# A trunk layer on one core: who adds the plain banks to the residual, the order of the next pair's loads, and where the weight sums pause

## The chip, the core and the metric

The kernel runs on one core of a Trainium2 chip. The metric is the time of one execution on the device in microseconds, lower is better. The core has five engines that run side by side, each with an instruction queue of its own that it works through in order: TensorE (PE in the profile; its weight loads are PEld), VectorE (DVE), ScalarE (ACT), GpSimd (POOL) and SyncE (SP), which here only starts transfers. An instruction waits in its queue until the semaphores of what it needs have come, and everything behind it on that engine waits too. Transfers that SP starts go through one queue (q1 in the profile), those that GpSimd starts through another (q0), and both share 16 DMA engines. Some of GpSimd's add to what is in the target (accumulating transfers).

## The reference, cut to what matters

The reference is one layer of a language model over 272 positions (16 meta tokens and 256 others), all in float32: a mixer (retention heads beside mLSTM heads), then a feed-forward part, then a last norm. The change lies in the feed-forward part:

```python
h = h + mix                                   # 272 x 2048
u = rmsnorm(h, norm_ffn)
up = causal_dwconv(u @ w_up, ffn_conv_w, ffn_conv_b)   # w_up: 2048 x 11264
gate, val = jnp.split(up, [5632], axis=-1)
h = h + (jax.nn.silu(gate) * val) @ w_down    # w_down: 5632 x 2048
return rmsnorm(h, norm_final)[:, 16:]         # 256 x 2048
```

## The kernel before

Float32 products are made of three reduced-precision ones. Every weight tile is loaded raw (`wraw`), ScalarE casts it to its high part `whi`, VectorE subtracts to get the rest `wlo` (together a split), and TensorE multiplies the activations' high part with both and their low part with `whi`. `whi` and `wlo` rotate through five buffers each, `wraw` through two homes of two tiles (`wraw0`, `wraw1`). Lines 140 and 142 (`split_w`) and 766 and 768 (`split`) are these splits.

Up to about 719 us the kernel makes the projections of the mixer (108 loads), its output (32 loads) and the first half of `w_up` (88 loads); a counter, `paced`, counts these loads. Then the last product follows for the first half of the 5632 rows of `w_down` (719 to 838 us), then the other 88 loads of `w_up`, then the second half of `w_down` (from 1091 us). I call the two `half` 0 and 1.

In one half the product with `w_down` runs over two pairs of column blocks of 512 (`b` = 0 and 2), and in each over eleven steps `q` of 256 rows each. Every step treats 2 tiles of 128 tokens and 2 blocks. Steps 0, 9 and 10 are plain: four products, 24 matmuls of 512 columns, accumulated into four PSUM banks `cs` (`atps` in the profile). Steps 1 to 8 use a scheme of seven products instead of eight for a 2 x 2 block product (`seven`, 21 matmuls): three into the banks `cs`, four into four more banks `ps` (`mmps`). VectorE makes one difference of weight tiles per step (line 830, `ta`) and four splits. The third combination of weight tiles, a sum of several, is not made on an engine: it is prepared in DRAM ahead of time.

These weight sums (class `Early`) are prepared while the projections run. Each of the 29 units has four parts: a copy of 512 KB from DRAM to DRAM (line 203, SP), and three accumulating transfers of 256 KB (lines 214 and 216, GpSimd). Which part starts after which load is set by the table `ahead`: part i after load 40 + 38 i / 16.

When the last seven-product step of a pair is done, `share` empties the four banks `ps`: it makes four combinations with ScalarE and VectorE in tiles of `x5` and adds each to its block of the residual `hn` by an accumulating transfer (`onto`, line 863). After the pair's last plain step ScalarE copies the four `cs` banks to tiles of `x5` (line 1000), and `onto` adds these to the same four blocks, but for the last pair of all, where VectorE adds straight from the banks. A copied bank is free for the next pair's plain step 0. The copies reuse tiles of `share`: the second to the fourth wait until its first to third transfer have landed.

The loads of the next steps are written into the same loop: `load_plain` (two raw tiles of 512 KB into a home of `wraw`) and `load_seven` (512 KB, 256 KB, and 256 KB of the prepared sum, into one of two buffers `left` made of `hT`). All go through SP's queue in the order written, by `load`. At a pair's end that is: step 10's plain tiles after step 8, step (2,2)'s after it, and after step 9 the next pair's plain step 0. A scheduler in the framework then orders each engine's instructions by its own estimate of times, so a change of the source also moves others.

Of the kernel before, what the change touches and what calls it, by code (L numbers as in the profile page):

```python
# [33 lines left out]
W0 = GW + 2 * P  # L34
WARM = 8

AHEAD, AHEAD_STEP = 40, 38

# [45 lines left out]
def trunk(ctx: ExitStack, tc: tile.TileContext, io, out: bass.AP):  # L86
    nc = tc.nc
# [132 lines left out]
    early = {u: Early(*u) for u in units}  # L220

    ahead = sorted((4 * n + 3 * i, n, i) for n in range(len(units)) for i in range(4))
    ahead = [(AHEAD + AHEAD_STEP * i // 16, early[units[n]].parts[p]) for i, (_, n, p) in enumerate(ahead)]


    mixp_cm = pool("mixp", 1, side="left")
# [530 lines left out]
    for half in range(2):  # L757
# [100 lines left out]
        def block(tt, b):  # L858
            return hn[:, tt, b * 512 : (b + 1) * 512]
# [49 lines left out]
        def load_plain(b, q, side, n=2):  # L909
            for j in range(b, b + n):  # L910
                raws[j, q] = raw_home([P, 2, 512], side)
                load(raws[j, q], io["wd"][j, half * NQD + q])

        def load_seven(b, q):

            nonlocal turn
            raw = left[turn]
            turn = 1 - turn
            load(raw[:, 2:4, :], io["wd7"][b // 2, half * NQD + q][:, 2:4, :])
            load(raw[:, 1, :], io["wd7"][b // 2, half * NQD + q][:, 1, :])  # L920
            load(raw[:, 0, :], early[b, half * NQD + q].kept[:, 0, :])
            homes[b, q] = raw
# [14 lines left out]
        for b in (0, 2):  # L937
            cs = {}
            for j in range(2):
                for tt in range(2):  # L940
                    cs[tt, j] = at.tile([P, 512], F32, name="atps")
            ps = [mm.tile([P, 512], F32, name="mmps") for _ in range(4)]

            final = half == 1 and b == 2
            steps = [0, 1, 6, 2, 7, 3, 4, 5, 8, 9, 10] if final else range(NQD)
            fast = [q for q in steps if q in FAST and not (final and q in BOTH)]
            plain = [q for q in steps if q not in fast]
            alone = plain[-lag:] if final else []
            if b == 0:
                load_plain(b, 0, 0)  # L950
                load_seven(b, 1)
                load_seven(b, 2)
            sums_home = [raw_home([P, 2, 512], 1) for _ in range(2)]
            load_sum(b, 1)
            load_sum(b, 2)
            for q in steps:
                if q in fast:
                    due = []
                    if final and q != fast[0]:
                        due, gains = gains[:1], gains[1:]  # L960
                    seven(b, q, cs, ps, q == fast[0], q == fast[-1], emptied, due)
                    if q == fast[-1]:
                        with tc.high_priority() if final else nullcontext():
                            shared = share(ps, b, final)
                else:
                    for j in range(1 if q in alone else 2):
                        w = split_step(raws.pop((b + j, q)))
                        for tt in range(2):
                            product(cs[tt, j], tt, q, w, q == plain[0], q == plain[-1 - (lag if final and (tt, j) == (1, 1) else 0)])

                if final:
                    if q == 0:
                        load_plain(b, 6, 0)
                    elif q == 6:
                        load_plain(b, 7, 0, 1)
                    elif q in (3, 4, 5):
                        load_plain(b, q + 5, 0 if q < 5 else 1, 1)
                    if q in (1, 2, 3):
                        load_seven(b, q + 2)
                        load_sum(b, q + 2)  # L980
                else:
                    if q == 6:
                        load_plain(b, 9, 0)
                    if q in range(1, 7):
                        load_seven(b, q + 2)
                        load_sum(b, q + 2)
                    if q == 8:
                        load_plain(b, 10, 1)
                    if b == 0:
                        if q in (7, 8):  # L990
                            load_seven(2, q - 6)
                        elif q == 9:
                            load_plain(2, 0, 0)
            for j in range(2):
                for n, tt in enumerate(range(2)):
                    c = (b + j) * 512
                    if not final:

                        x = x_tile((4, 3, 1, 0)[2 * j + n])
                        emptied = nc.scalar.copy(x, cs[tt, j])  # L1000
                        onto(tt, b + j, x)
                        if half == 1:
                            gains.append((tt, b + j, c, c + 512))
                    elif j == 0:
                        add(cs[tt, j], tt, c)
                        squares(tt, b, c, c + 512)
                        times_gain(tt, c, c + 512)
# [111 lines left out]
```

## Time and profile before

| what | value |
| --- | --- |
| median of 3 runs | 1219.86 us (1217.63 to 1221.83) |
| profiled execution, its own time | 1222.59 us |
| its span, first to last instruction | 1220.8 us |
| mean granted TensorE clock | 0.994 |
| instructions | 23064 |
| read from and written to memory | 268.59 MB, 42.47 MB |

Line 1000 runs twelve times, first at 776.6 and last at 1154.4 us; line 863 issues 27 transfers, 256 KB each, with a median of 8.3 us from issue to landing. In a row of the timeline the columns are: start and length in us, engine, line, operation, what it writes and reads, how often, and in brackets how long the engine had been idle before it and what ended that. In a row of a line's view the three numbers after the name are the shortest, median and longest length in ns, then come the first and the last start in us. In a row of waits stand the total in us, the number of waits and the longest. In a row of stretches stand, for each engine, the busy us and the number of instructions, then the granted clock, the busy share of the DMA engines and what they moved. Several matmuls overlap, so the distance between starts is what one costs, not its length.

### The profile page before, as it was taken

What the parts mean: (1) busy time and instruction counts of PE and PEld (TensorE: products, weight loads), DVE (VectorE), ACT (ScalarE), POOL (GpSimd) and SP (SyncE); (2) the same over time, 40 slices, a digit from 0 to 9 for tenths busy, and PEclk for the clock granted to TensorE, in tenths of its full rate; (3) what the DMA queues carried; (4) which work ended last, traced back from release to release, by engine and by line L of the source; (5) the groups of instructions that cost most, each with busy time, mean ns of one, the idle gap of its engine ahead of it and who ended that gap; (6) DMA issues with size and microseconds to landing.
All of it is one profiled execution on the core that took longest, in us unless ns stands there. A gap on an engine that the chain in (4) does not pass through costs nothing.

```text
span 1220.8 us, 23064 instructions
## 1 busy us (share of the span) xinstructions
PE 1202.5 (99%) x8947; PEld 1154.5 (95%) x8947; DVE 943.0 (77%) x1378; ACT 712.9 (58%) x973; POOL 270.1 (22%) x361
## 2 busy tenths in 40 slices
PE   9999999999999999999999999999999999999897
PEld 9999999999999999999999998788999999998686
DVE  8877878767765766788888779795877777779686
ACT  8657756656557556555555556564655555556573
POOL 0100022222221331232213200303232232210232
PEclk9999999999999999999999999999999999999899
DMA  8764677777886877778777867969988778858866
GB/s 276 269 214 157 209 231 216 236 217 223 235 234 179 260 231 222 227 245 243 222 229 223 234 198 250 268 216 284 275 264 243 222 230 224 227 183 290 236 205 181
DMA packets 104094, 281.64 MB, mean 231 GB/s; under 512 B 16624, under 2 KB 20848, under 8 KB 103856
## 3 DMA queue, kind: packets, MB, share of 16 engines
q1 hardware_dynamic: 84016, 239.06, 57.7%
q0 software_dynamic: 19392, 40.26, 18.5%
q8 instruction: 70, 1.15, 0.4%
q10 hardware_dynamic: 576, 0.85, 0.2%
q14 instruction: 40, 0.33, 0.1%
HBM read 268.59 MB, written 42.47 MB: 255 GB/s over the span
## 4 chain that ended last, share of the span: by engine, by line
PE 94%; DMA 4%; DVE 1%; ACT 1%; issue 0%; DVEq 0%; SPq 0%; ACTq 0%
PE mmps L149 25%; PE mmps L152 25%; PE mmps L150 25%; DMA wraw<-in_wd 2%; PE mmps L844 2%; PE mmps L845 2%; PE mmps L847 2%; PE atps L845 1%; PE atps L844 1%; PE atps L819 1%; PE atps L822 1%; PE atps L820 1%; PE atps L847 1%; DMA wraw<-in_wu 1%; DMA hT<-kept 1%; PE atps L442 1%
## 5 line engine op out<-in xcount | busy, mean ns | idle before, releaser
L140 ACT CAST whi<-wraw 128x1024 fp32r<-128x1024 f32 x346 | 361.9, 1049 | 355.8 <-PE mmps L150 226.9
L142 DVE TENSOR_TENSOR wlo<-wraw,whi 128x1024 fp32r<-128x1024 f32 x346 | 429.9, 1244 | 104.4 <-ACT whi L140 99.4
L149 PE MATMUL mmps<-uh,whi 128*128 128x258 f32 x1408 | 345.2, 283 | 2.9 <-ACT whi L140 2.9
L150 PE MATMUL mmps<-ul,whi 128*128 128x258 f32 x1408 | 344.9, 281 | 0.0
L149 PEld LDWEIGHTS mmps<-uh,whi 128*128 128x128 f32 x1408 | 265.3, 188 | 3.3 <-ACT whi L140 3.1
L150 PEld LDWEIGHTS mmps<-ul,whi 128*128 128x128 f32 x1408 | 266.8, 190 | 0.1
L149 PE MATMUL mmps<-xh,whi 128*128 128x272 f32 (+2 forms) x864 | 219.8, 288 | 0.0
L150 PE MATMUL mmps<-xl,whi 128*128 128x272 f32 (+2 forms) x864 | 218.4, 285 | 0.0
L152 PE MATMUL mmps<-uh,wlo 128*128 128x258 f32 x1408 | 197.9, 283 | 0.0
L152 PEld LDWEIGHTS mmps<-uh,wlo 128*128 128x128 f32 x1408 | 181.6, 190 | 0.0
L150 PEld LDWEIGHTS mmps<-xl,whi 128*128 128x128 f32 x864 | 162.8, 188 | 0.0
L149 PEld LDWEIGHTS mmps<-xh,whi 128*128 128x128 f32 x864 | 162.7, 188 | 0.1
L209 POOL TENSOR_TENSOR pace<-whi 128x1 f32<-128x1 f32 x87 | 52.0, 598 | 407.4 <-ACT whi L140 407.4
L152 PE MATMUL mmps<-xh,wlo 128*128 128x272 f32 (+2 forms) x864 | 126.9, 285 | 0.0
L152 PEld LDWEIGHTS mmps<-xh,wlo 128*128 128x128 f32 x864 | 114.6, 188 | 0.0
L695 DVE TENSOR_TENSOR cu<-mmps,rstd 128x258 f32<-128x258 f32 x88 | 37.5, 426 | 68.9 <-PE mmps L152 68.4
L768 DVE TENSOR_TENSOR wlo<-hT,whi 128x1024 fp32r<-128x1024 f32 x58 | 71.3, 1247 | 6.5 <-ACT whi L766 6.2
L766 ACT CAST whi<-hT 128x1024 fp32r<-128x1024 f32 x58 | 59.7, 1050 | 15.2 <-DMA hT<-kept 4.6
L766 ACT CAST whi<-wraw 128x1024 fp32r<-128x1024 f32 (+1 forms) x58 | 46.6, 836 | 32.7 <-DVE wraw L830 21.4
L150 PE MATMUL mmps<-mixl,whi 128*128 128x258 f32 x256 | 63.1, 283 | 0.0
L149 PE MATMUL mmps<-mixh,whi 128*128 128x258 f32 x256 | 62.5, 283 | 0.0
L768 DVE TENSOR_TENSOR wlo<-wraw,whi 128x1024 fp32r<-128x1024 f32 (+1 forms) x58 | 53.2, 953 | 1.9 <-PE mmps L847 0.8
(271 smaller groups left out, 1775.7 us busy)
## 6 DMA issues: line engine op xcount, KB each, us to landing
wraw<-in_wu SPq DMA_DIRECT2D x176, 512.0 KB, 4.5
wraw<-in_wi SPq DMA_DIRECT2D x108, 512.0 KB, 4.4
wraw<-in_wo SPq DMA_DIRECT2D x32, 512.0 KB, 4.5
wraw<-in_wd SPq DMA_DIRECT2D x30, 512.0 KB, 6.0
kept<-in_wd SPq DMA_DIRECT2D x29, 512.0 KB, 6.5
kept<-in_wd POOLq DMA_DIRECT2D x58, 256.0 KB, 6.3
hT<-in_wd SPq DMA_DIRECT2D x29, 512.0 KB, 5.1
kept<-kept POOLq DMA_DIRECT2D x29, 256.0 KB, 5.3
```

Of the source, the lines that this page charges most:

```text
L140: nc.scalar.copy(hi, raw)
L142: nc.vector.tensor_tensor(out=lo, in0=raw, in1=hi.bitcast(F32), op=ALU.subtract)
L149: nc.tensor.matmul(ps, hi[:, k, :], xh(kk), start=kk == first, stop=False)
L150: nc.tensor.matmul(ps, hi[:, k, :], xl(kk), start=False, stop=False)
L152: nc.tensor.matmul(ps, lo[:, k, :], xh(kk), start=False, stop=kk == last)
L209: with tc.issue_after(nc.gpsimd.tensor_tensor(out=pace, in0=x, in1=x, op=ALU.add).ins):
L695: evacuated = nc.vector.tensor_tensor(out=u, in0=ps[:, :NQ], in1=rstd2, op=ALU.mult)
L766: copied = nc.scalar.copy(hi, x)
L768: return copied, nc.vector.tensor_tensor(out=lo, in0=x, in1=hi.bitcast(F32), op=ALU.subtract)
L844: nc.tensor.matmul(o, sh[:, f, m, :], hi[:, i, :], start=begin, stop=False)
L845: nc.tensor.matmul(o, sl[:, f, m, :], hi[:, i, :], start=False, stop=False)
L847: nc.tensor.matmul(o, sh[:, f, m, :], lo[:, i, :], start=False, stop=end)
```

## The change

Three edits. First, after a pair's last plain step the copies are added to `hn` by VectorE, no longer by accumulating transfers. Second, in the first pair's loop, the loads of step (2,2) are written after those of the next pair's plain step 0, not before. Third, the table of the weight sums: parts start every 22 / 10 loads instead of every 38 / 16, and what would come at load 222 or later comes 16 loads later, so that no part starts between loads 222 and 238. The border of the halves is load 228.

```diff
-AHEAD, AHEAD_STEP = 40, 38
+AHEAD, AHEAD_STEP, REST, RESUME = 40, 22, 222, 238
...
-    ahead = [(AHEAD + AHEAD_STEP * i // 16, early[units[n]].parts[p]) for i, (_, n, p) in enumerate(ahead)]
+    at_load = (AHEAD + AHEAD_STEP * i // 10 for i in range(len(ahead)))
+    ahead = [(a if a < REST else a + RESUME - REST, early[units[n]].parts[p]) for a, (_, n, p) in zip(at_load, ahead)]
...
                     if b == 0:
-                        if q in (7, 8):
-                            load_seven(2, q - 6)
+                        if q == 7:
+                            load_seven(2, 1)
                         elif q == 9:
                             load_plain(2, 0, 0)
+                            load_seven(2, 2)
...
                         emptied = nc.scalar.copy(x, cs[tt, j])
-                        onto(tt, b + j, x)
+                        nc.vector.tensor_tensor(out=block(tt, b + j), in0=block(tt, b + j), in1=x, op=ALU.add)
```

What this does to the engines' order is shown at three places. Lines behind the table are numbered one or two higher in the new kernel, those behind the copies three higher.

SP's queue in half 0 at the end of the first pair, before: `wraw1` are the plain tiles of step 10, `wraw0` those of the next pair's step 0, and the three rows of `hT` step (2,2), the last of them its prepared sum.

```order
L907 DMA wraw1_9517<-in_wd 128x1024
L907 DMA wraw1_9519<-in_wd 128x1024
L907 DMA hT_72<-in_wd7 128x1024
L907 DMA hT_72<-in_wd7 128x512
L907 DMA hT_72<-kept2_2_89 128x512
L907 DMA wraw0_9556<-in_wd 128x1024
L907 DMA wraw0_9558<-in_wd 128x1024
```

And of the change:

```order
L909 DMA wraw1_9522<-in_wd 128x1024
L909 DMA wraw1_9524<-in_wd 128x1024
L909 DMA wraw0_9558<-in_wd 128x1024
L909 DMA wraw0_9560<-in_wd 128x1024
L909 DMA hT_72<-in_wd7 128x1024
L909 DMA hT_72<-in_wd7 128x512
L909 DMA hT_72<-kept2_2_89 128x512
```

The two plain tiles moved ahead of three transfers, 1 MB. The same holds in half 1.

VectorE's queue at the same border, before: the splits of the next pair's plain step 0 (`wraw0`), then those of step (2,1), whose `ta` stands ahead of them.

```order
L830 TENSOR_TENSOR wraw1_9608<-hT_72 128x1024
L142 TENSOR_TENSOR wlo_9614<-wraw0_9556,whi_9612 128x1024
L142 TENSOR_TENSOR wlo_9630<-wraw0_9558,whi_9628 128x1024
L768 TENSOR_TENSOR wlo_9646<-hT_72,whi_9645 128x1024
L768 TENSOR_TENSOR wlo_9656<-hT_72,whi_9655 128x1024
```

And of the change:

```order
L143 TENSOR_TENSOR wlo_9619<-wraw0_9558,whi_9617 128x1024
L832 TENSOR_TENSOR wraw1_9613<-hT_72 128x1024
L143 TENSOR_TENSOR wlo_9635<-wraw0_9560,whi_9633 128x1024
L1004 TENSOR_TENSOR hn_4814<-hn_4814,x5_5926 128x512 x4
L770 TENSOR_TENSOR wlo_9651<-hT_72,whi_9650 128x1024
L770 TENSOR_TENSOR wlo_9661<-hT_72,whi_9660 128x1024
```

The four adds stand between the splits of the plain step and those of step (2,1). Each waits for ScalarE's copy and for the landing of the transfer that `share` sent to the same block. On ScalarE the four copies now stand together behind both casts of the plain step; before, two stood between the casts and two behind.

SP's queue at the border of the halves, before: the last plain tiles, the first tiles of `w_up`'s second half, and the copy that begins a weight sum (`kept0_17`).

```order
L907 DMA wraw1_9985<-in_wd 128x1024
L907 DMA wraw1_9987<-in_wd 128x1024
L126 DMA wraw0_10066<-in_wu 128x1024
L126 DMA wraw0_10159<-in_wu 128x1024
L203 DMA kept0_17_101<-in_wd7 256x512
L126 DMA wraw1_10096<-in_wu 128x1024
L126 DMA wraw1_10129<-in_wu 128x1024
```

And of the change:

```order
L909 DMA wraw1_9990<-in_wd 128x1024
L909 DMA wraw1_9992<-in_wd 128x1024
L127 DMA wraw0_10071<-in_wu 128x1024
L127 DMA wraw0_10162<-in_wu 128x1024
L127 DMA wraw1_10101<-in_wu 128x1024
L127 DMA wraw1_10132<-in_wu 128x1024
```

The sum's copy is gone from there: it now starts ten loads before the half's end. The tile behind it, `wraw1_10096`, is the second that TensorE needs. GpSimd's three accumulating transfers of weight sums that were issued around this border move too, and so do the weight sums between all other loads.

## The prediction

> **What bounds the kernel now.** I read four views, in this order: the page (which engine is full), the list of waits of the matmul engine (when it is not full), a table by stretches around those waits, and the timeline at them. L-numbers are lines of the kernel before.
>
> ```profile
> PE 1202.5 (99%) x8947; PEld 1154.5 (95%) x8947; DVE 943.0 (77%) x1378; ACT 712.9 (58%) x973; POOL 270.1 (22%) x361
> PE atps L819 <- ACT x L1000: 5.9, 2, 3.8
> PE mmps L149 <- ACT whi L140: 2.9, 1, 2.9
> ```
>
> TensorE (PE) is busy for 99% of the span, so only what holds PE up can be won. Apart from the first microsecond and the tail there are three such places. I call them A, C and B: two waits for a copy out of a plain bank (L1000), 2.1 and 3.8 us, and one of 2.9 us for a split weight tile.
>
> ```profile
> core 0: us, PE busy (x) PEld busy (x) DVE busy (x) ACT busy (x) POOL busy (x), PEclk, DMA share, GB/s
> 400.00:420.00 20.00, 20.00 (x168) 20.00 (x168) 14.72 (x18) 10.12 (x14) 5.61 (x8) 1.00 0.91 276
> 775.00:782.00 7.00, 4.86 (x15) 3.77 (x15) 3.28 (x3) 5.85 (x9) 3.52 (x4) 0.76 1.02 226
> 782.00:824.00 42.00, 42.00 (x182) 33.78 (x181) 41.24 (x41) 28.91 (x34) 3.37 (x7) 1.00 0.72 232
> 838.00:841.00 3.00, 0.14 (x1) 0.14 (x2) 0.16 (x1) 1.24 (x2) 0.04 (x1) 1.00 1.08 306
> 1148.40:1157.40 9.00, 5.29 (x13) 4.19 (x14) 3.84 (x4) 6.40 (x9) 3.54 (x4) 0.62 0.95 233
> 1157.40:1206.00 48.60, 48.60 (x210) 39.13 (x209) 43.13 (x41) 29.78 (x40) 16.64 (x15) 1.00 0.71 213
> ```
>
> A lies at 775 us (half 0, first to second column pair), B at 838 us (half 0 to half 1), C at 1148 us (half 1, first to second pair). At A and C the granted clock (PEclk) is also down, at B it is not. In 782 to 824 us, the step run behind A, VectorE (DVE) is busy for 41.24 of 42.00 us: there it is as full as PE.
>
> ```profile
> 775.65 1.04 ACT L140 CAST whi<-wraw 128x1024 fp32r<-128x1024 f32 x1 [6.84 <-DMA wraw<-in_wd]
> 776.61 1.06 ACT L1000 COPY x<-atps 128x512 f32<-128x512 f32 x2
> 777.24 0.50 PE L819 MATMUL atps<-whi,mh 128*128 128x512 f32 x1 [2.14 <-ACT x L1000]
> 784.49 0.39 PE L844 MATMUL atps<-whi,sh 128*128 128x512 f32 x1
> 786.35 0.63 PE L847 MATMUL atps<-wlo,sh 128*128 128x512 f32 x2
> 1152.12 0.80 PE L819 MATMUL atps<-whi,mh 128*128 128x512 f32 x1 [3.76 <-ACT x L1000]
> 1160.10 0.40 PE L844 MATMUL atps<-whi,sh 128*128 128x512 f32 x1
> ```
>
> The name in the wait is not the cause. ScalarE (ACT) stood 6.84 us before a cast of the next pair's first plain tile, waiting for its load; the copies that free PE's banks are queued behind that cast. PE stopped at 777.24 - 2.14 = 775.1 us. What A cost is read from where the next step begins: eight matmuls take 786.35 - 784.49 = 1.86 us, 0.233 each, so the 24 of plain step 0 take 5.6 us, and the seven-product step behind it could begin at 780.7 instead of 784.49. **A costs 3.8 us** (2.1 of waiting, 1.7 of slow clock). At C PE stopped at 1148.4, could begin that step at 1154.0 and did at 1160.1: **C costs 6.1 us**. **B costs 2.9.** Together 12.8 us; more cannot come from these borders.
>
> **The change part by part.** First the plain loads, now ahead of the second step's.
>
> ```profile
> L907 SPq DMA_DIRECT2D wraw<-in_wd x2: 627/948/1269, 764.0 to 765.3; - x2
> ...
> DMA to landing us min/median/max: 11.6/12.2/12.8
> L907 SPq DMA_DIRECT2D hT<-kept x1: 702/702/702, 763.2 to 763.2; - x1
> ...
> DMA to landing us min/median/max: 9.8/9.8/9.8
> L907 SPq DMA_DIRECT2D hT<-kept x1: 394/394/394, 1137.5 to 1137.5; - x1
> ...
> DMA to landing us min/median/max: 10.3/10.3/10.3
> L907 SPq DMA_DIRECT2D wraw<-in_wd x2: 395/407/419, 1138.0 to 1138.5; - x2
> L1000 ACT COPY x<-atps x12: 577/588/592, 776.6 to 1154.4; 128x512 f32<-128x512 f32 x12
> ```
>
> At A the two tiles land at 775.6 and 778.1 us. Ahead of them in SP's queue stands 1 MB of step (2,2), three transfers, of which the last (`hT<-kept`) lands at 763.2 + 9.8 = 773.0. The plain tiles are 1 MB too. In that place the second of them lands when the step's last transfer did: 773.0 at A, 1137.5 + 10.3 = 1147.8 at C. At A both casts (1.04 us) are over by 774.1, before PE needs anything: A's wait goes. At C the second cast ends at 1148.9, and the new order has all four copies behind both casts; the first copy (0.59) ends at 1149.4, 1.1 us after PE stopped: **at C 1.1 of the 6.1 stays**. The bounds of this are 0 (the tile lands 1.1 earlier) and 6.1. Step (2,2)'s loads, moved back, take the plain tiles' landing, 778.1 at A; VectorE asks for them four splits after its start (below), past 783: hidden.
>
> Second, the adds. Twelve `hn<-x` transfers of GpSimd's queue become twelve VectorE adds.
>
> ```profile
> L863 POOL DMA_DIRECT2D hn<-x x4: 857/889/1032, 763.7 to 768.8; - x4
> ...
> DMA to landing us min/median/max: 8.9/9.3/10.1
> L863 POOL DMA_DIRECT2D hn<-x x4: 859/888/1137, 1137.4 to 1142.8; - x4
> ...
> DMA to landing us min/median/max: 10.2/10.4/11.4
> L878 DVE TENSOR_TENSOR hn<-hn,x x1: 681/681/681, 1202.3 to 1202.3; 128x512 f32<-128x512 f32 x1
> 781.17 1.22 DVE L768 TENSOR_TENSOR wlo<-hT,whi 128x1024 fp32r<-128x1024 f32 x1 [0.69 <-ACT whi L766]
> ```
>
> One such add stands in the trace, 0.68 us, so four cost 2.7. Worse than their length is what they wait for: each adds to a block to which `share` has just sent an accumulating transfer, and must wait until that has landed. The last of the four is issued at 768.8 and lands within 10.1 us, by 778.9 at A; at C by 1142.8 + 11.4 = 1154.2. Behind the fourth add in VectorE's queue stand the splits of the seven-product step (the order rows of the change), and PE waits for those. At A the first of them starts at 778.9 + 0.7 = 779.6 and is done at 780.8 (before: 781.17, done 782.4). PE wants it eight matmuls into the step, at 780.7 + 1.9 = 782.6 (before 786.35). The lead of VectorE over PE falls from 4.0 to 1.8 us.
>
> ```profile
> L830 DVE TENSOR_TENSOR wraw<-hT x7: 1215/1217/1220, 786.3 to 818.3; 128x1024 f32<-128x1024 f32 x7
> 819.65 1.57 ACT L766 CAST whi<-wraw 128x1024 fp32r<-128x1024 f32 x2 [0.44 <-PE mmps L847]
> 821.12 0.39 PE L844 MATMUL mmps<-whi,sh 128*128 128x512 f32 x1
> ```
>
> And that lead is used up on the way: L830 runs once per step, six steps in 818.3 - 786.3 = 32.0 us, so VectorE needs 5.33 us a step where PE needs 21 x 0.233 = 4.9. At the end of the run the first of the two casts is ready at 819.65 + 1.05 = 820.7 and used at 821.12: 0.4 us are left. With 2.2 us less to start from, PE pays 2.2 - 0.4 = **1.8 us of A's 3.8 back**. Bounds: 0, if VectorE makes it up, and 3.8, if the landings slip by 2 more. At C the step needs its first split at 1154.0 + 1.1 + 1.9 = 1157.0; it is done at 1154.2 + 0.7 + 1.2 = 1156.1, a lead of 0.9, and the last pair has only five such steps, with plain steps between: in 1157.4 to 1206 us VectorE had 5.5 us free. No price there.
>
> Third, the weight sums, kept away from the border of the halves and paced at 2.2 instead of 2.375 loads a part.
>
> ```profile
> L203 SPq DMA_DIRECT2D kept<-in_wd x1: 501/501/501, 825.2 to 825.2; - x1
> ...
> DMA to landing us min/median/max: 12.2/12.2/12.2
> 839.76 1.04 ACT L140 CAST whi<-wraw 128x1024 fp32r<-128x1024 f32 x1 [5.47 <-DMA wraw<-in_wu]
> 840.86 0.39 PE L149 MATMUL mmps<-uh,whi 128*128 128x258 f32 x1 [2.93 <-ACT whi L140]
> ```
>
> The sum's first transfer lands at 825.2 + 12.2 = 837.4; the tile queued behind it lands at 839.7, 2.3 us later, and PE had wanted its split from 840.86 - 2.93 = 837.9 on. A load of 512 KB thus takes at least 2.3 us of this queue here, and the transfer that goes is of 512 KB as well, so the tile comes 2.3 us earlier or more (the transfer is written to memory too, and was in flight for 12.2). With 2.9 earlier, a cast of 1.0 included, the wait is gone. I take 2.9, since the two tiles' splits stand ahead of three of the four adds in the new order; the bounds are 2.3 and 2.9. The denser pace elsewhere adds 8% to the sums; PE stayed full (20.00 of 20.00) in a stretch with the DMA engines at 0.91, so I price it at 0, with bounds 0 and 1.
>
> **Sum:** A 3.8 - 1.8 = 2.0, B 2.9, C 6.1 - 1.1 = 5.0: 9.9 us. The profiled execution took 1222.59 us, which gives 1212.7. It is 2.7 above the median of the three runs shown and 0.8 above the slowest. I cannot tell whether that surplus sits in the slow clock that goes or in the profiling, and start halfway, from 1221: **1211 us**.
>
> **A rule on the clock.** At A the clock fell to half after 2.1 us of waiting, at C after 3.8; at B it stayed at 1.00 after 2.9. The Trainium skill, "TensorE: Matmul & The Clock Gate", section "What's actually happening", says that the array drops to half rate after an idle window of about 3.4 us that runs freely. The drop at A after 2.1 us disagrees with that length, the difference between A and B fits a window that runs freely. By a strict 3.4 us A's slow clock would not hang on its wait, its 1.7 us would stay, and the sum would be 8.2, 1213.
>
> **The rivals.** Slower: VectorE's queue held by the landings. It decides at the fourth landing of A and C. Each microsecond L beyond 778.9 and 1154.2 costs one at A and, past the lead of 0.9, one at C: L = 2 leaves 9.9 - 2 - 1.1 = 6.8 (1214). L = 4 leaves 2.8, and there the new waits reach 2.1 us, from which A lost clock, so 1.7 and 2.3 (C's 6.1 less 3.8) go again: -1.2, no gain, 1222. L = 6 costs 9.9 - 6 - 5.1 - 4.0 = -5.2: 1226. For it speaks that these landings took 8.9 to 11.4 us; against it that the transfers ahead keep their places and that later ones are dropped.
>
> The loads don't come earlier, because the homes they fill are freed only by VectorE's splits of step 9: then only B is won, 1218. Against it: at C both were issued by 1138.5, long before landing.
>
> The slow clock has another cause than the waits: it stays at A alone (1.7; 8.2, 1213) or at both (1.7 and 2.3; 5.9, 1215). For it speaks B, where as long a wait left the clock at 1.00; against it, that in the stretches quoted it is low at these two waits alone. The first of the two is what the Trainium skill's window, taken strictly, would make of it.
>
> **How the numbers follow.** Forecast 0.58 (1208 to 1213); landings late by about 2 us 0.15, by 4 or more 0.06; loads not earlier 0.08; clock slow at A alone 0.05, at both 0.04; the rest 0.04. A measurement of this kernel can tell about 0.3% from no change, 3.7 us, so faster means below 1216.2: the forecast, 1214, 1213, 1215 and half the rest, 0.58 + 0.15 + 0.05 + 0.04 + 0.02 = 0.84. Same: 1218, and a hundredth each of the late landings and the rest, 0.10. Slower: what is left of these, 0.06. The low end is 1219.86 - 12.8 = 1207, the whole of A, B and C off the median; the high end, 1217, takes in the late landings of 2 us and the slow clock, and leaves out 0.16 above.
>
> **What would show it.** Right: no PE wait for a copy at A (under 0.5 us), about 1 us at C, PEclk 1.00 at both; no PE wait at B; VectorE's adds waiting for `hn<-x`, and PE waits of some 1.8 us in all in the second half of the step run behind A. Wrong: a PE wait over 2 us at the first seven-product step of a second pair (landings), the casts of the first plain tiles still waiting past PE's last product (loads), or PE waits in the up projection (pace).

## The result, and the profile after

| what | before | after |
| --- | --- | --- |
| median of 6 runs each, on one chip | 1220.66 us (1217.63 to 1224.04) | 1211.97 us (1211.57 to 1213.42) |
| ratio | | 0.9932, 95% interval 0.9913 to 0.9952 |
| profiled execution, its own time | 1222.59 us | 1212.01 us |
| its span | 1220.8 us | 1210.2 us |

The change makes the kernel faster by 0.7%, 8.7 us between the medians and 10.6 us between the profiled executions; 1211 us was forecast. The runs also lie closer together: they cover 1.9 us after and 6.4 before.

The same views as before, of the kernel after. First the engines' busy time and the waits of the matmul engine from 0.5 us on (total, number, longest, in us), where waits of 5.9 and 2.9 us stood. (Lines are numbered one or two higher than before: L768 and L770 are the splits of a seven-product step, L846 to L849 its matmuls, L821 to L824 those of a plain step, L1003 the copies, L1004 the adds, L909 the loads, L832 the tile `ta`.)

```profile
PE 1198.8 (99%) x8947; PEld 1150.3 (95%) x8947; DVE 951.6 (79%) x1390; ACT 713.4 (59%) x973; POOL 258.7 (21%) x349
PE atps L263 <- DVE ones L237: 1.2, 1, 1.2
PE atps L846 <- ACT whi L768: 0.8, 1, 0.8
PE mmps L150 <- ACT whi L141: 0.6, 1, 0.6
```

No wait for a copy is left among them (the first row is the start of the kernel). The table by stretches of the kernel after, A within the second row, the step run behind A in the third, B in the fourth, C in the fifth:

```profile
core 0: us, PE busy (x) PEld busy (x) DVE busy (x) ACT busy (x) POOL busy (x), PEclk, DMA share, GB/s
400.00:420.00 20.00, 20.00 (x168) 20.00 (x168) 14.86 (x18) 10.35 (x15) 7.13 (x10) 1.00 0.97 283
768.00:780.00 12.00, 12.00 (x53) 9.62 (x53) 8.75 (x10) 7.54 (x10) 2.87 (x4) 1.00 0.94 264
782.00:824.00 42.00, 41.03 (x172) 31.72 (x172) 39.99 (x40) 25.90 (x30) 4.14 (x7) 1.00 0.66 223
824.00:840.00 16.00, 15.44 (x91) 13.44 (x90) 9.86 (x13) 8.25 (x11) 2.60 (x3) 1.00 0.97 278
1140.00:1150.00 10.00, 10.00 (x44) 7.78 (x43) 7.36 (x9) 6.56 (x9) 0.86 (x2) 1.00 1.07 324
```

PE is full and its clock 1.00 at A and C. What is lost now is lost in the step run behind A (41.03 of 42.00) and, a little, at B. VectorE, full there before (41.24), has two us free in the same stretch: remember this row.

Now A in the timeline of the kernel after: casts and copies of ScalarE, adds and splits of VectorE, and the first matmul of the seven-product step. In brackets stands how long the engine was idle before the row, and what ended that.

```profile
771.90 1.05 ACT L141 CAST whi<-wraw 128x1024 fp32r<-128x1024 f32 x1 [1.70 <-DMA wraw<-in_wd]
773.15 1.08 ACT L1003 COPY x<-atps 128x512 f32<-128x512 f32 x2 [0.20 <-PE atps L824]
774.13 1.29 DVE L1004 TENSOR_TENSOR hn<-hn,x 128x512 f32<-128x512 f32 x2
776.22 0.59 ACT L1003 COPY x<-atps 128x512 f32<-128x512 f32 x1 [1.08 <-DMA hn<-x]
776.24 0.69 DVE L1004 TENSOR_TENSOR hn<-hn,x 128x512 f32<-128x512 f32 x1 [0.82 <-DMA hn<-x]
778.27 0.69 DVE L1004 TENSOR_TENSOR hn<-hn,x 128x512 f32<-128x512 f32 x1 [1.34 <-DMA hn<-x]
778.88 2.35 DVE L770 TENSOR_TENSOR wlo<-hT,whi 128x1024 fp32r<-128x1024 f32 x2
780.42 0.39 PE L846 MATMUL atps<-whi,sh 128*128 128x512 f32 x1
```

The plain tile's cast is over before the copies are wanted, and these now wait for PE, not for a load. The adds wait for the landings of `share`'s transfers (`hn<-x`), as forecast. The fourth copy on ScalarE waits for such a landing as well (776.22), because the tile that it writes is still being sent. The casts of the seven-product step stand behind it.

Where the gain lies is read from the starts of marked matmuls in the two traces. A loss "behind A" is the time from the first matmul of the seven-product step there to the first of plain step 9, less 0.2333 us for each matmul between them (165 in the kernel's new order, 167 in the old one; 0.2333 is (780.42 - 764.55) / 68, a stretch without a wait). At C, PE wants the first copy when the four matmuls ahead of it are through, 4 x 0.2333 us after the first of them (1147.26 before, 1142.72 after).

| mark | before | after | gained since the last mark | forecast |
| --- | --- | --- | --- | --- |
| first plain step of half 0 | 718.94 | 718.82 | 0.1 | |
| A: first seven-product step | 784.49 | 780.42 | 3.95 | 3.8 |
| loss behind A | 0.0 | 2.1 | -2.1 | -1.8 |
| B: PE goes on in the up projection | 840.86 | 836.54 | 2.35 | 2.9 |
| C: PE wants the first copy | 1148.2 | 1143.65 | 0.2 | 0 |
| C: first seven-product step | 1160.10 | 1149.48 | 6.1 | 5.0 |
| end of the span | 1220.8 | 1210.2 | 0 | 0 |

### The profile page after: what moved, and what is told of

It is laid out like the page before. It is cut to its first block, busy times and chain, and to the rows that moved or that the text cites. A ratio compares the mean times of both kernels' runs of the same rounds, so it can differ in the third digit from the quotient of the medians.

```text
span 1210.2 us, 23069 instructions
## 1 busy us (share of the span) xinstructions
PE 1198.8 (99%) x8947; PEld 1150.3 (95%) x8947; DVE 951.6 (79%) x1390; ACT 713.4 (59%) x973; POOL 258.7 (21%) x349
## 4 chain that ended last, share of the span: by engine, by line
PE 95%; DMA 2%; DVE 1%; ACT 0%; issue 0%; SPq 0%; DVEq 0%; ACTq 0%
PE mmps L150 25%; PE mmps L153 25%; PE mmps L151 25%; PE atps L821 2%; PE mmps L849 2%; PE atps L822 2%; PE atps L824 2%; PE mmps L846 2%; PE mmps L847 2%; PE atps L846 1%; PE atps L847 1%; PE atps L849 1%; DMA wraw<-in_wu 1%; DVE wlo L770 1%; DMA hT<-kept 1%; PE atps L444 1%
## 5 line engine op out<-in xcount | busy, mean ns | idle before, releaser
L770 DVE TENSOR_TENSOR wlo<-hT,whi 128x1024 fp32r<-128x1024 f32 x58 | 69.3, 1218 | 3.5 <-ACT whi L768 3.5
L768 ACT CAST whi<-hT 128x1024 fp32r<-128x1024 f32 x58 | 59.3, 1049 | 15.7 <-DMA hT<-kept 5.3
L768 ACT CAST whi<-wraw 128x1024 fp32r<-128x1024 f32 (+1 forms) x58 | 46.6, 835 | 35.5 <-DVE wraw L832 17.7
L770 DVE TENSOR_TENSOR wlo<-wraw,whi 128x1024 fp32r<-128x1024 f32 (+1 forms) x58 | 53.2, 952 | 1.5 <-ACT whi L768 0.5
```

Of the source, the lines that this page charges most:

```text
L768: copied = nc.scalar.copy(hi, x)
L770: return copied, nc.vector.tensor_tensor(out=lo, in0=x, in1=hi.bitcast(F32), op=ALU.subtract)
```

## The experiments

**First group: the three edits apart.** Each kernel ran beside the kernel before on one chip (25 runs of it, median 1220.11 us, 1216.71 to 1224.39).

`e1_loads`: the second edit alone.

```diff
                     if b == 0:
-                        if q in (7, 8):
-                            load_seven(2, q - 6)
+                        if q == 7:
+                            load_seven(2, 1)
                         elif q == 9:
                             load_plain(2, 0, 0)
+                            load_seven(2, 2)
```

> The kernel before with the second edit alone (step (2,2)'s loads behind the next plain step's); the accumulating transfers and the weight sums' table stay. Theory: the loads alone win A and C. No PE wait for a copy at 775 or 1148 us above 0.5 us, clock 1.00 there; without the adds VectorE's lead at the first seven-product step behind A stays near 4 us, so nothing is given back there, and the whole 3.8 of A and 5.9 of C are won: 9.7 us less than before. The wait at B stays at 2.9. Rival 1: B grows by what A wins, since the tile behind the weight sum lands when the DMA engines get to it (busy 1.03 in 824 to 840 us before), not earlier: B 2.9 + 3.8 = 6.7, total gain 5.9. Rival 2: the adds are what frees the copies, so A and C stay and the gain is under 2.

Measured: 1217.06 us (1212.32 to 1219.34), ratio 0.9967 (0.9949 to 0.9985). From its list of waits and its table by stretches, around B:

```profile
PE mmps L149 <- ACT whi L140: 4.2, 1, 4.2
PE atps L819 <- ACT x L1001: 0.8, 1, 0.8
775.00:782.00 7.00, 7.00 (x31) 5.63 (x31) 3.75 (x4) 5.56 (x8) 2.58 (x3) 1.00 1.10 255
836.00:842.00 6.00, 2.84 (x13) 2.84 (x14) 1.47 (x2) 3.35 (x5) 2.74 (x4) 0.58 1.05 274
```

A is gone without the adds, and so is C but for 0.8 us: the loads do it, and rival 2 falls. Rival 1 holds in kind: the wait at B is longer, 4.2 us instead of 2.9 (6.7 was expected), and the clock falls there to 0.58. At the first matmul of half 1's product the kernel stands at 1091.87 against 1091.52 before: what A gave is gone by then. Of A's 4.06 us, 1.1 were lost behind A, where the expectation had nothing, and the rest around B. VectorE's lead at the first seven-product step (from the end of its first split there to when PE wants it) is 2.8 us, not the 4 that was expected without the adds. Its span is 5.4 us shorter, near the rival's 5.9; the medians differ by 3.1. At C it gains the 5.9 (from 1097.47 to 1154.56, before from 1097.12 to 1160.10).

`e2_adds`: the first edit alone (the last two lines of the diff of the change).

> The kernel before with the first edit alone (VectorE's adds in place of twelve accumulating transfers). Theory: no gain, since the waits at A and C are for loads: the PE waits for a copy stay at about 2.1 and 3.8 us, clock down at both, B at 2.9; VectorE has four adds of 0.68 more behind A, of which PE pays 0 to 1.8 in the step run: 0 to 1.8 us slower than before. Rival: twelve transfers of 256 KB less on GpSimd's queue bring the loads earlier and the time falls by 2 or more.

Measured: 1219.39 us (1217.12 to 1222.07), ratio 1.0003 (0.9991 to 1.0015). No gain, as expected; the rival is out. Its profiled execution waited less than that of before for the copies (0.5 at A, 2.4 at C) and lost 1.65 us behind A. I put the shorter waits down to the scatter between executions, since the median didn't follow.

`e3_rest`: the third edit alone.

> The kernel before with the third edit alone (the weight sums' table). Theory: B's wait falls from 2.9 to 0.6 or less and nothing else changes: 2.3 to 2.9 us less than before, PE 20.00 of 20.00 in 400 to 420 us, the waits at A and C stay at 2.1 and 3.8 within 0.5. Rival: the denser pace takes DMA time from loads elsewhere, and the gain is under 1.

Measured: 1215.52 us (1214.13 to 1217.88), ratio 0.9972 (0.9961 to 0.9984), 3.4 us by the ratio. Its wait at B is gone altogether (PE 10.00 of 10.00 us in 830 to 840); copies were waited for twice, 4.2 us together (1.4 at A, 2.8 at C; 2.1 and 3.8 within 0.5 were expected). It loses 1.0 us behind A, without the adds.

`e4_onto`: the second and third edit, with the accumulating transfers back.

```diff
-                        nc.vector.tensor_tensor(out=block(tt, b + j), in0=block(tt, b + j), in1=x, op=ALU.add)
+                        onto(tt, b + j, x)
```

> The kernel of the change with the accumulating transfers back in place of VectorE's adds (so the second and third edit alone). Theory of the prediction: the adds cost about 1.6 to 1.8 us of PE's time behind A and win nothing, so this kernel is 1.6 to 1.8 us faster than the change (some 12 us less than before), the lead of VectorE at the first seven-product step behind A is above 3.5 us and PE loses nothing in the step run behind it. Rival: the small PE stalls behind A come from the loads of step 9 and the last seven-product steps, which land at 809 to 816 us with or without the adds: then this kernel has the same stalls and is within 0.7 of the change. Second rival: the twelve transfers take DMA time back, and the wait at C returns by 1 us or more: slower than the change by 1 or more.

Measured: 1211.64 us (1211.13 to 1212.14, 4 runs), ratio 0.9939 (0.9922 to 0.9957). It loses 1.4 us behind A (the theory had nothing), the change 2.1, and waits 1.1 us for a copy at C. VectorE's lead is 3.2 us (above 3.5 was expected): its first split starts at 778.45, hardly sooner than in the change (778.88). So the median is that of the change, and the first rival of this run is the nearest: most of the loss behind A is there **without** the adds. That made the forecast's reason for it doubtful, and the second group was built on that.

**Second group: what is lost behind A.** In the trace of the change PE's longest wait behind A is at 815.87 us, and it ends on a load: the tile of step 8 landed at 814.7, its cast ran from 814.77 to 815.82. The view of the loads' line, kept to the three transfers of step 8 in the change, says how long they were in flight:

```profile
L909 SPq DMA_DIRECT2D hT<-in_wd x2: 328/328/328, 806.2 to 807.3; - x2
...
DMA to landing us min/median/max: 8.1/8.3/8.5
```

Ahead of them in SP's queue stand the two plain tiles of step 9, 1 MB, issued at 802.85 and 803.31 and needed only at 821.

`e8_again`: the change itself once more, as the group's measure.

> The kernel of the change once more, unaltered, as the measure for the three others of this group. Median 1211.5 to 1212.5, all runs within 1211 to 1213.5; in the trace no PE wait for a copy at A, at most 1.2 us at C, some 1.6 us lost in the step run behind A, 0 to 1 us of waiting at B. If the waits for a copy at C in the runs without the adds (0.8 and 1.1 us against 0.1 in the change) came by chance and not from the adds, this profile may show up to 1 us at C as well.

Measured: 1211.69 us (1210.13 to 1212.81), ratio 0.9935 (0.9918 to 0.9952). Its profile loses 1.85 us behind A and waits 1.4 us for a copy at C, where the first profile of the same kernel shows none above 0.2.

`e5_late9`: step 9's loads behind step 8's.

```diff
-                    if q == 6:
-                        load_plain(b, 9, 0)
                     if q in range(1, 7):
                         load_seven(b, q + 2)
                         load_sum(b, q + 2)
+                    if q == 6:
+                        load_plain(b, 9, 0)
```

> The change with one more move: in every pair the two plain tiles of step 9 are loaded behind the three transfers of step 8 instead of ahead of them. Theory: what is lost behind A is the landing of step 8's tile (814.7 us, 8.5 in flight behind 1 MB of step 9; PE waits 1.0 us there); behind the move it lands some 3 us earlier, the loss behind A falls from 1.6 to 0.6 or less, the rest stays: 0.7 to 1.3 us faster than the change. Rival, the prediction's step: VectorE's used-up lead is what is lost behind A, so PE waits as much as before at the following splits: no difference (within 0.4). Second rival: step 9's tiles now land too late and PE waits for them by more than 0.5 us: slower.

Measured: 1210.14 us (1209.33 to 1211.00), ratio 0.9924 (0.9907 to 0.9941). Step 8's transfers in this kernel, then the stretch behind A and VectorE's line of `ta` in it:

```profile
L909 SPq DMA_DIRECT2D hT<-in_wd x2: 328/328/328, 805.9 to 807.0; - x2
...
DMA to landing us min/median/max: 4.0/4.5/4.9
782.00:824.00 42.00, 42.00 (x181) 33.50 (x180) 41.35 (x42) 26.53 (x31) 5.00 (x8) 1.00 0.73 232
L832 DVE TENSOR_TENSOR wraw<-hT x7: 1215/1217/1220, 782.6 to 813.9; 128x1024 f32<-128x1024 f32 x7
```

The kernel is 1.55 us faster than `e8_again`, a little more than the 0.7 to 1.3 of the theory. The transfers land after 4.5 us instead of 8.3, PE is full (loss 0.25 us), and this with the same adds in the same place. VectorE, which stood idle for 2 us behind A in the change, is busy again, 41.35 of 42.00. It needs (813.9 - 782.6) / 6 = 5.22 us a step, PE 4.9, so its lead over PE does shrink by 0.3 us a step. It is 2.4 us at the first step and used up at 812.2, where PE waits for the cast of a `ta`; that is the whole loss of 0.25 us, so the lead all but suffices. The theory holds, the prediction's step doesn't.

`e6_late9_onto`: the same, with the accumulating transfers in place of the adds.

> The same move with the accumulating transfers back in place of VectorE's adds. Theory: the loss behind A goes altogether (under 0.3 us), since VectorE's lead is near 4 us and the landing of step 8 no longer binds; at C a wait of about 1 us for a copy stays. If the adds cost VectorE's lead, this kernel is 0.3 to 0.8 us faster than the move with the adds; if the accumulating transfers' traffic behind A delays loads as much, within 0.3; if it is slower by 0.5 or more, the adds were a gain.

Measured: 1209.90 us (1208.35 to 1210.44), ratio 0.9919 (0.9901 to 0.9938). It loses 1.2 us behind A, more than the kernel with the adds: the theory of "under 0.3" is wrong for this kernel. Two waits make up 1.1 of it, and they are VectorE's. The first of them, with VectorE's queue ahead of it (the second, at 813.51, looks the same):

```profile
799.51 1.22 DVE L770 TENSOR_TENSOR wlo<-hT,whi 128x1024 fp32r<-128x1024 f32 x1
800.64 1.22 DVE L832 TENSOR_TENSOR wraw<-hT 128x1024 f32<-128x1024 f32 x1
801.97 1.57 ACT L768 CAST whi<-wraw 128x1024 fp32r<-128x1024 f32 x2 [2.81 <-DVE wraw L832]
803.08 0.50 PE L846 MATMUL mmps<-whi,sh 128*128 128x512 f32 x1 [0.21 <-ACT whi L768]
```

PE waits for the cast of a `ta`, the cast for the `ta`, and the `ta` for its turn behind a split, with no gap on VectorE. VectorE's lead at the first step was 2.5 us, not near 4: its first split starts at 778.91, as late as with the adds, because ScalarE's copies wait for `share`'s transfers here too, and at 790.2 VectorE stood 0.9 us for a load. So taking the adds away frees little of VectorE's lead. By the medians adds and transfers are worth the same here, within 0.3 us.

`e7_more_adds`: VectorE's work at the borders doubled, in the change.

```diff
                         nc.vector.tensor_tensor(out=block(tt, b + j), in0=block(tt, b + j), in1=x, op=ALU.add)
+                        nc.vector.tensor_tensor(out=x, in0=x, in1=x, op=ALU.add)
```

> The change with VectorE's work at each border doubled: behind each of the twelve adds one more of the same size (x + x into x, which nothing reads; no part of the result), 2.7 us more of VectorE's time at each of the three borders, of which 2.0 stands ahead of the first seven-product split at A. Theory of the prediction: behind A VectorE has no slack, so each us of lead lost is paid by PE: the loss behind A grows from 1.6 to 4 us or more, and the kernel is 2.4 to 3 us slower than the change. Rival: the loads' landings set the pace behind A, VectorE catches up while it waits for them, and the kernel is under 1 us slower.

Measured: 1213.44 us (1211.73 to 1214.13), ratio 0.9949 (0.9932 to 0.9966): 1.75 us more than the change beside it, between the two expectations. Of 2.7 us more work behind A, PE lost 0.7 more there (2.6 against 1.85); another 0.85 us was lost behind C, up to the end of the span. Its stretch behind A:

```profile
782.00:800.00 18.00, 17.64 (x76) 13.78 (x75) 17.88 (x19) 10.60 (x13) 1.61 (x3) 1.00 0.77 247
800.00:824.00 24.00, 22.92 (x96) 17.55 (x95) 23.48 (x24) 15.23 (x18) 2.51 (x4) 1.00 0.64 212
```

Here VectorE is full from the start (17.88 of 18.00) and PE waits before 800 us already, for casts of a `ta`. The lead at the first step fell by 0.5 us only (1.6 against 2.15), since the first two of the new adds at A fill time in which VectorE waits for landings anyway. The run is not a pure test: the added work also moved the order of VectorE's queue, and three of PE's four waits are at a `ta` that now stands behind a split. The two limits lie beside each other: the later of "VectorE's part is done" and "the load has landed" counts, and they don't add up.

**Third group: the pause by itself, and what is left at C.** The kernel before had 17 runs here, median 1220.33 us.

`e10_rest_only`: the pause at the old pace.

```diff
-    ahead = [(AHEAD + AHEAD_STEP * i // 16, early[units[n]].parts[p]) for i, (_, n, p) in enumerate(ahead)]
+    at_load = (AHEAD + AHEAD_STEP * i // 16 for i in range(len(ahead)))
+    ahead = [(190 + (a - 190) * 2 // 3 if 190 <= a < 238 else a, early[units[n]].parts[p]) for a, (_, n, p) in zip(at_load, ahead)]
```

> The kernel before with the pause alone, at the old pace: parts of the weight sums that would start at loads 190 to 237 start at 190 to 221, the others where they did, 38 / 16 loads apart. Theory: B's wait is the sums' transfers near the border, so this kernel has the same gain as the whole third edit (3.4 us, interval 2.0 to 4.8, in its own run) and PE waits at most 0.6 us for a split at B. Rival: the edit's gain came from its pace, which ends the sums earlier and moves all the others; then this kernel gains under 1.5 us.

Measured: 1215.48 us (1212.55 to 1221.02), ratio 0.9967 (0.9952 to 0.9982), 4.0 us by the ratio; PE is busy for 10.00 of 10.00 us in 830 to 840. The pause is what wins at B, and the pace wins and costs nothing that these runs can tell (between loads 190 and 221 this kernel's parts start closer together than in either of the others). Not all of the 4.0 us need be B's: the profiled execution, the fastest of its 12, does not wait for a copy at A at all, though its loads stand in the old order, and loses 2.1 us behind A, without the adds.

`e9_copies`: on top of `e5_late9`, the first three copies ahead of the second plain tile's cast, the adds behind both splits.

```diff
-                        w = split_step(raws.pop((b + j, q)))
+                        with tc.issue_after(third.ins) if j == 1 and b == 2 and q == plain[0] else nullcontext():
+                            w = split_step(raws.pop((b + j, q)))
+                        while waiting and j == 1 and b == 2:
+                            y, x = waiting.pop(0)
+                            with tc.issue_after(parted_w.ins):
+                                nc.vector.tensor_tensor(out=y, in0=y, in1=x, op=ALU.add)
...
-                        nc.vector.tensor_tensor(out=block(tt, b + j), in0=block(tt, b + j), in1=x, op=ALU.add)
+                        if (j, n) == (1, 0):
+                            third = emptied
+                        if b == 0:
+                            waiting.append((block(tt, j), x))
+                        else:
+                            nc.vector.tensor_tensor(out=block(tt, b + j), in0=block(tt, b + j), in1=x, op=ALU.add)
```

(`third` is the third copy, `parted_w` VectorE's part of the last split.)

> The kernel with step 9's loads moved, and at a pair's end one more order: ScalarE makes the first three copies out of the plain banks ahead of the cast of the second plain tile (before and in the change, the copies that free the banks stand behind a cast whose load comes late), and VectorE's adds stand behind both plain splits. Theory: the wait for a copy that is left at C (0.1 to 1.5 us in the profiles so far) is the second tile's landing passed on by ScalarE's queue; with the copies ahead of that cast PE waits for no copy (under 0.3 us) and the kernel is 0.2 to 1.0 us faster than the one without this order. Rival: the first tile's own split or the second's, now later, is what PE waits for next, by as much: no difference, or slower.

> The kernel with step 9's loads moved, once more, to stand beside the one with the copies ahead: median 1209.8 to 1210.6, under 0.3 us lost behind A, a wait for a copy at C of 0.1 to 1.5 us.

Measured: `e9_copies` 1211.66 us (1210.87 to 1213.17), ratio 0.9932 (0.9915 to 0.9949); `e11_late9_again` 1209.62 (1209.26 to 1211.23), ratio 0.9915 (0.9898 to 0.9932), with no wait for a copy at C this time. The order did what was meant, no wait for a copy stands in its list, but PE waits behind A instead:

```profile
PE mmps L847 <- ACT whi L769: 0.7, 2, 0.4
782.00:824.00 42.00, 41.21 (x175) 32.27 (x174) 41.66 (x42) 26.18 (x31) 4.14 (x7) 1.00 0.75 237
```

VectorE gets its second split and the adds later, and has no slack behind A. The kernel is 2.0 us slower than the one without this order; the loss behind A (1.6 us against 0.5 in `e11_late9_again`, where under 0.3 was expected) accounts for 1.1 of it. Another 1.0 us lies behind C's first seven-product step (61.75 us from there to the end against 60.75), most of it at one wait for a plain tile's cast at 1193.67. The forecast for this order was wrong.

**The best version** is `e5_late9`: its 11 runs have a median of 1210.09 us, the change's 12 runs one of 1211.88. `e6_late9_onto` (1209.90, 6 runs) can't be told apart from it.

## Why the prediction was right

The time was forecast at 1211 and is 1212; the mechanisms at A, B and C were right. Step by step:

- **The loads at A: right.** 3.8 was forecast, 3.95 gained. The second plain tile landed at 771.8, forecast 773.0. That the loads alone do it is shown by `e1_loads`; in all nine profiles with the new order PE waits for no copy at A. How much there is to gain scatters: in the four profiles with the old order the wait is 2.1, 1.4, 0.5 and 0 us at A and 3.8, 2.8, 2.4 and 1.7 at C. The prediction priced both at the first of these, the largest.
- **The adds wait for landings: right.** The last landed at 778.2 and the first split behind it started at 778.88 (forecast 778.9 and 779.6); VectorE's lead at the first step was 2.2 us (forecast 1.8; 4.0 before). But the adds are only part of why it fell: without them, and with the loads in the new order, it is 2.8 (`e1_loads`), 3.2 (`e4_onto`) and 2.5 us (`e6_late9_onto`), since ScalarE's copies wait for landings too.
- **"PE pays 1.8 of A's 3.8 back": right in size, wrong in its cause.** 2.1 us are lost behind A. The step that failed is the one from the lead to the loss, that with less to start from PE must pay what is missing. With the same adds `e5_late9` loses 0.25 and `e11_late9_again` 0.5. Without them `e4_onto` loses 1.4. The 0.4 us that the prediction counted as left were read at the last `ta`, which before stood behind a split of its step (818.3 us, the split at 817.2); after, it stands ahead of both, 1.1 us sooner in VectorE's queue. What came late was step 8's load, behind 1 MB of step 9 that nobody needed yet: some 1.5 of the 2.1 us lie at the two waits that its transfers end (815.87 and 818.56). Before the change the same transfers took up to 7.6 us, and PE did not wait, because it wanted the tile 4 us later than after the change, which issues it only 2.8 us earlier (806.15 instead of 808.95). VectorE's part of the loss is not nothing in every kernel: where its queue is fuller or ordered otherwise (`e6_late9_onto`, `e7_more_adds`), PE pays for it. The prediction named VectorE's queue as "what is late next" and left SP's queue in that stretch unexamined. The sign it had named, PE waits of some 1.8 us behind A, came true and could not tell the two causes apart; the row of stretches could, in which VectorE had become idle.
- **B: right in kind, 0.55 too large.** 2.9 was forecast (bounds 2.3 to 2.9), 2.35 gained. The tile behind the dropped sum was in flight for 8.6 us instead of 11.8 and its cast still came 0.6 us late. The pause is the cause, not the pace (`e10_rest_only`).
- **C: right, with scatter.** 5.0 was forecast, 6.1 gained: the 1.1 us that were to stay are 0.1 in this execution. In other profiles with the same order of loads and copies the wait for a copy there is 0.0, 0.2, 0.5, 0.8, 0.8, 1.1 and 1.4 us. The term was sound as a typical value; one execution doesn't show it.
- **The pace at 0: right.** PE is full between the borders, and 0.2 us were gained on the way, where nothing was forecast.
- **The sum of A, B and C: right only because all three were made together.** The prediction added them as if each stood alone. `e1_loads` shows that A's gain would have been lost by the end of B: behind a transfer that lands when it lands, PE only waits longer. B's edit had to free B for A's gain to pass.
- **The base.** The 25 runs of before in the first group answer what was left open: those of 1220.1 us and more have a mean granted clock of 0.994 or 0.995, those below 0.996 or 0.997. The surplus of the profiled execution goes with its slow clock, and so it went with the waits. The later runs of before divide less cleanly (runs of 1220.1 to 1222.2 us stand there at 0.996 and 0.997, and one of 1219.7 at 0.995), so the clock is not all of it. The forecast gain of 9.9 us was priced on this slow execution; the medians gained 8.7. That the time came out within 1 us is in part luck: half the surplus was a guess, B was 0.55 too large and C 1.1 too small.

The rivals: the late landings did not come (lead 2.2 us), the loads did come earlier, and the clock is 1.00 at both places, so the slow clock hung on the waits. The Trainium skill, "TensorE: Matmul & The Clock Gate", section "What's actually happening", puts the drop to half rate behind an idle window of about 3.4 us, one of windows that run freely. The traces agree with freely running windows: the clock changes at marks 3.413 us apart (last section). They disagree if a window must be idle from end to end, as the prediction's strict reading had it: 2.14 us of 3.41 were enough at A, and its slow clock went with its wait.

## What to carry to other kernels

When an edit lets the bounding engine reach a stretch sooner, go through every queue of that stretch for what is issued relative to it, the load queue first: a prefetch that was early enough before may now stand in front of the transfer that is needed next. Price gains at several places of one chain together, not one by one, since a wait for a transfer downstream can swallow what was won upstream. To tell which of two late parties sets a wait, move the one that costs nothing to move: a loss of the forecast size is no proof of the forecast cause. And follow a wait to its end before naming it: taking a suspect away, as `e4_onto` and `e6_late9_onto` do with the adds, tests little if something else holds the same engine to nearly the same time.

## What the runs showed of the hardware

Whether a wait costs the clock depends on where it lies, not only on its length. In every profile of this study the granted clock changes only at marks of one grid, 3.413 us apart. Before, the falls at A and C lie at 778.30 and 1150.35 us, 109 such steps apart, and the clock is down for one step and for two. The kernel before, cut at these marks (A, then B, then C; the first number after the stretch's length is PE's busy time, the third from the end the clock):

```profile
774.89:778.30 3.41, 1.27 (x6) 0.88 (x6) 1.23 (x1) 2.15 (x4) 0.82 (x2) 1.00 1.10 273
778.30:781.71 3.41, 3.41 (x10) 2.65 (x9) 1.77 (x2) 3.41 (x5) 2.69 (x4) 0.50 0.96 188
836.33:839.74 3.41, 1.60 (x14) 1.39 (x12) 0.00 (x0) 0.00 (x0) 0.00 (x0) 1.00 1.09 306
839.74:843.15 3.41, 2.29 (x19) 2.29 (x20) 1.23 (x1) 2.86 (x4) 2.19 (x3) 1.00 1.09 290
1146.94:1150.35 3.41, 1.41 (x7) 0.79 (x5) 0.00 (x0) 0.00 (x0) 0.00 (x0) 1.00 1.09 290
1150.35:1153.77 3.42, 1.66 (x4) 1.37 (x5) 1.23 (x1) 2.77 (x4) 1.41 (x2) 0.50 0.81 233
1153.77:1157.18 3.41, 3.41 (x9) 2.65 (x9) 2.39 (x3) 3.41 (x6) 2.13 (x3) 0.50 1.00 206
```

In the step ahead of each fall PE was idle for 2.14 and 2.00 of 3.41 us. B's wait of 2.93 us is longer than A's, but lies across a mark: 1.81 us in one step and 1.12 in the next, and the clock did not fall. Over all profiles, the kernels' first microseconds and tails aside, a clock that was up fell behind each of the six steps with 1.9 to 2.4 us idle (also in `e1_loads`, twice in `e2_adds`, and in `e3_rest`) and behind none with 1.81 or less. It rose again after the first step in which PE was busy throughout; 0.88 us idle in one step of `e3_rest` kept it down. The fall cost 1.7 us at A, half a step, and 2.3 at C.

The marks lie differently in each execution: the clock's first rise, from which they count, comes between 4.1 and 7.4 us. So the same wait of two or three us can cost the clock in one execution and not in the next. That may be part of why the kernel before scatters over 7.7 us (25 runs) and the change over 3.3 (12 runs). This reading was not tested by itself.
